# Recurrent scores with 64 stationary columns and a value half in groups of 512 columns: one kernel, two edits

## The chip, the cores and the metric

The kernel runs on one core of a Trainium2 chip. Its time is the device time of one execution in microseconds. The matrix engine (TensorE), the vector engine (VectorE), the scalar engine (ScalarE), GpSimd and the DMA queues run side by side and wait for each other through semaphores. In the rows below, PE is TensorE's matmul, PEld its loading of the stationary operand, DVE is VectorE, ACT ScalarE, POOL GpSimd, and SP the engine whose queue issues the loads.

## What is computed

One step of a two-layer decoder on 1024 prompt tokens and 64 sample tokens (8 sequences of 8), width 1024. Layer 0 has a convolution branch and a recurrent branch with 8 heads; layer 1 gates through a mixing of positions. Cut to the two places that the change touches:

```python
# layer 0, per head, chunks of 64 tokens: c = 64, n = 16
scores = jnp.einsum('bnthd,bnshd->bnhts', qf * jnp.exp(bcum - b_mid), k * jnp.exp(b_mid - bcum))
scores = jnp.where(causal, scores, 0.0)
o_intra = jnp.einsum('bnhts,bnshv->bnthv', scores, vf)

# layer 1: w_in is 1024 x 6144; columns 0..2047 are u, 2048..4095 are v, the rest the gate
z = _rmsnorm(x, g_norm) @ w_in
uv = jax.nn.gelu(z[..., :2 * D_C])
gate = z[..., 2 * D_C:]
u = uv[..., :D_C]
v = _layernorm(uv[..., D_C:], ln_g, ln_b)       # over the 2048 columns
mix = jnp.einsum('hts,bnshd->bnthd', ws, vp) + b_s
y = (u * mix * jax.nn.silu(gate)) @ w_out
```

## The kernel before

**Products.** Every large product is taken in float32r with both operands split into a high and a low part: three matmuls (high x high, high x low, low x high) for each of the 8 slices of the contraction. ScalarE makes the high part of a weight piece (`wh`), VectorE the low part (`wl`), from a raw piece of 512 KB that SP's queue loads. Two buffers hold raw pieces (pool `wrp`), three hold split pieces (pool `whp`), and `ft` is a pool of 31 large tiles for everything else. The list `wspecs` names the pieces in the order of use; `wget` takes the next ones and splits two (`AHEAD`) beyond them.

**Layer 0** is written in the order in which its instructions are to run. Weights are the stationary operand, and tokens stream in three pieces of 368, 352 and 368 columns. Between the pieces, generators add the small steps of the recurrent heads. `states(h, g)` does half `g` of head `h`: 512 tokens, four blocks of 128, each block two chunks of 64. For each block, one fp32 matmul makes the 128 x 128 scores of both chunks (line 729: 128 keys stationary, 128 queries moving) and a second one overwrites the corner in which the queries of the second chunk meet the keys of the first, with other scalings (line 730: 64 keys stationary, 64 queries moving). VectorE then copies the causal part into a tile that is zero elsewhere. `decode(h)` does the same for the sample tokens (line 790, 64 x 64), and for half 0 its scores stand right behind those of `states`.

**Layer 1's value half** begins once layer 0's output is summed. From here on a scheduler sets the order on all engines but SP, whose loads stay in the order of the text. Here the tokens are the stationary operand (128 of them) and the weights stream: `token_unit` (lines 503 to 505) takes a group of 256 weight columns as two pieces of 4 x 256 columns, and for each of 8 token blocks makes 24 matmuls with 256 columns into one PSUM tile. A ninth unit, the tail (lines 512 to 515), does the 64 sample tokens: a tile that holds their high and low parts side by side is stationary, and matmuls with 128 and with 64 stationary columns alternate. There are 8 groups. Each block is evacuated through a gelu on ScalarE and a statistics instruction on VectorE; four blocks make a tile that goes to DRAM (`va_d`, `vb_d`, and `vs_d` for the sample). After the first group a sum over columns is broadcast to all partitions (`rsqrt_bcast`, lines 1131 to 1133): three matmuls, three square roots on ScalarE, three reciprocals on VectorE. Later, `head_load(h)` loads the 256 columns of a head back, and the u and gate units of layer 1 run with weights stationary again.

**The end** (lines 1315 to 1317) is the one place that already takes weight pieces of 2 x 512 columns; those are kept in `ft` tiles (`fwh`, `fwl`).

Of the kernel before, what the change touches and what calls it, by code (L numbers as in the profile page):

```python
# [9 lines left out]
F32 = mybir.dt.float32  # L10
F32R = mybir.dt.float32r
I32 = mybir.dt.int32
AF = mybir.ActivationFunctionType
ALU = mybir.AluOpType

P = 128
# [4 lines left out]
NS = NSB * NSS  # L21
T = NPR + NS
KD = D // P
# [12 lines left out]
def kernel(  # L36
# [9 lines left out]
    cst = ctx.enter_context(tc.tile_pool(name="cst", bufs=1))  # L46
# [7 lines left out]
    def ft(name, dt=F32, shape=(P, T)):  # L54
        return ftp.tile(list(shape), dt, tag="ft", name=name)

    def ta(name, shape, dt=F32):
        return smp.tile(list(shape), dt, tag="a", bufs=5, name=name)
# [10 lines left out]
    def th(name, shape, dt=F32):  # L69
        return smp.tile(list(shape), dt, tag="h", bufs=6, name=name)  # L70

    def ps_mm(name):
        return mmp.tile([P, 512], F32, tag="mm", name=name)

    def ps_ax(name):
        return axp.tile([P, 512], F32, tag="ax", name=name)

    def dscr(name, n, w=T, p=P):
        return [tc.dram_tile([p, w], F32, name=f"{name}{i}") for i in range(n)]

    load = nc.sync.dma_start
    store = nc.scalar.dma_start
# [12 lines left out]
    tt_op = counted(nc.vector.tensor_tensor)  # L95
# [5 lines left out]
    act = nc.scalar.activation  # L101
    mm = nc.tensor.matmul
# [18 lines left out]
    w0, w1 = w_in_ab[0], w_in_c[0]  # L121
    wo0, wo1 = w_out_ab[0], w_out_c[0]
# [4 lines left out]

    def wload(spec):
        kind, w2d, rws, c0 = spec
        shape = {"u": [P, 8, P], "h": [P, 4, 256], "q": [P, 2, 512]}[kind]  # L130
        nk, nc_ = shape[1:]
        raw = wrp.tile(shape, F32, tag="wr", name="wr")
        load(out=raw, in_=w2d[rws * P:(rws + nk) * P, c0:c0 + nc_].rearrange("(k p) c -> p k c", p=P))
        return raw, shape

    def wsplit(rw, final=False):
        raw, shape = rw
        if not final:
            hi = whp.tile(shape, F32R, tag="wh", name="wh")
            lo = whp.tile(shape, F32R, tag="wl", name="wl")  # L140
        else:
            hi, lo = ft("fwh", F32R, shape), ft("fwl", F32R, shape)
        split(hi, lo, raw)
        return hi, lo

    VAL, GLU, AGT, QC, FC, IC, BGT = (1024 * i for i in range(7))
    wspecs = []
# [4 lines left out]
    def plan_h(w2d, c0, r0=0, n=2):  # L152
        for q in range(n):
            wspecs.append(("h", w2d, r0 + 4 * q, c0))
# [17 lines left out]
    for part in (2, 3, 0, 1):  # L172
        for mg in range(4):
            plan_h(wo0, mg * 256, 4 * part, 1)
    for g in range(8):
        plan_h(w1, 2048 + 256 * g)
    for h in range(8):
        for d in range(2):
            plan_u(w1, (2 * h + d) * P)
# [8 lines left out]
    wspecs = deque(wspecs)  # L188
# [11 lines left out]
    def wget(n=1, ahead=None):  # L200
        prefetch(n if here["manual"] else n + AHEAD)
        wuse[0] = n
        return [wready.popleft() for _ in range(n)]
# [183 lines left out]
    tail = ft("tail", F32R, (P, KD, P))  # L387
# [97 lines left out]
    def token_unit(ah, al, tail, evac):  # L485
# [43 lines left out]
        else:  # L529
            evac(8, NS, last())  # L530

    def act_evac(dst, func):
        return lambda a, n, ps: act(out=dst[:, a:a + n], in_=ps, func=func)

# [178 lines left out]
    def states(h, g):  # L713
        d = hd[h]
        k2, q2, sm, vr, o_t = d["k2"], d["q2"], d["sm"], vrows[h // 2], d["o"]
        hs = slice((h % 2) * P, (h % 2) * P + P)
        gs = slice(g * 512, (g + 1) * 512)
        for _ in range(g * LAG):
            yield
        q4, k3 = th("q4", [P, 8, 64]), th("k3", [P, 8, 64])  # L720
        for dst, src, r in ((k3, k2, 1), (q4, q2, 0)):
            tt_op(out=dst, in0=src[:, gs].rearrange("p (c s) -> p c s", s=64),
                  in1=sm[:, r, 8 * g:8 * g + 8, None].to_broadcast([P, 8, 64]), op=ALU.mult)
        for _ in range(LAG):
            yield
        sc = ps_ax("sc")
        for b in range(4):
            cs = slice((4 * g + b) * P, (4 * g + b + 1) * P)
            mm(sc[:, b * P:(b + 1) * P], k2[:, cs], q2[:, cs], start=True, stop=True)  # L729
            mm(sc[0:64, b * P + 64:(b + 1) * P], k3[:, 2 * b, :], q4[:, 2 * b + 1, :], start=True, stop=True)  # L730
        yield
        vpred(out=sct[g], mask=mcaus[:, None, :].to_broadcast([P, 4, P]),
              data=sc.rearrange("p (b t) -> p b t", b=4))
        for b in range(4):
            act(out=k3[:, 2 * b, :], in_=k3[:, 2 * b, :], func=AF.Copy, scale=sm[:, 2, 8 * g + 2 * b + 1:8 * g + 2 * b + 2])
        kp = ps_ax("kp")
        for b in range(4):
            nc.tensor.transpose(kp[:, b * P:(b + 1) * P],
                                k3[:, 2 * b:2 * b + 2, :].rearrange("p c s -> p (c s)"), ident)
        yield  # L740
        kt = th("kt", [P, 512])
        act(out=kt, in_=kp, func=AF.Copy)
        dp = ps_ax("dp")
        for b in range(4):
            mm(dp[:, b * P:(b + 1) * P], kt[:, b * P:(b + 1) * P], vr[4 * g + b][:, hs], start=True, stop=True)  # L745
        for b in range(4):
            act(out=q4[:, 2 * b + 1, :], in_=q4[:, 2 * b + 1, :], func=AF.Copy,
                scale=sm[:, 2, 8 * g + 2 * b:8 * g + 2 * b + 1])
        yield
        s_in = []  # L750
        for b in range(4):
            s_p = d.get("s")
            s_in.append(s_p)
            s_n = tb("Sn", [P, P])
            dpb = dp[:, b * P:(b + 1) * P]
            if s_p is None:
                vcopy(out=s_n, in_=dpb)
            else:
                stt(out=s_n, in0=s_p, scalar=sm[:, 3, 4 * g + b:4 * g + b + 1], in1=dpb,
                    op0=ALU.mult, op1=ALU.add)  # L760
            d["s"] = s_n
        op = ps_ax("op")
        for b in range(4):
            bs = slice(b * P, (b + 1) * P)
            mm(op[:, bs], vr[4 * g + b][:, hs], sct[g][:, b, :], start=True, stop=s_in[b] is None)  # L765
            if s_in[b] is not None:
                mm(op[:, bs], s_in[b], q4[:, 2 * b:2 * b + 2, :].rearrange("p c s -> p (c s)"),  # L767
                   start=False, stop=True)
        yield
        act(out=o_t[:, g * 512:(g + 1) * 512], in_=op, func=AF.Copy)  # L770
        if g == 1:
            store(out=hgrn_prompt[0, 0, h], in_=d["s"])
        d["done"] += 1
# [367 lines left out]
    rsqrt_cols(rc[0:NS, 8:9], mp[0:NS, 8:9], 1.0 / D)  # L1141
    rb = ft("rb")
    tail = tails(xh, xl)
    va_d = dscr("va_d", 8, 1024)
    vb_d = dscr("vb_d", 8, 1024)
    vs_d = dscr("vs_d", 8, 256, NS)
    bst = cst.tile([P, 9, 8, 6], F32, name="bst")
    for g in range(8):
        va = ft("va", F32, (P, 4, 256))
        vb = ft("vb", F32, (P, 4, 256))  # L1150
        vs = ta("vs", [NS, 256])

        def evac(t, n, ps):
            dst = vs if t == 8 else (va, vb)[t // 4][:, t % 4, :]
            act(out=dst, in_=ps, func=AF.Gelu_apprx_tanh, scale=rc[0:n, t:t + 1])
            nc.vector.bn_stats(out=bst[0:n, t, g, :], in_=dst)

        token_unit(xh, xl, tail, evac)
        store(out=va_d[g], in_=va.rearrange("p a b -> p (a b)"))
        store(out=vb_d[g], in_=vb.rearrange("p a b -> p (a b)"))  # L1160
        store(out=vs_d[g], in_=vs)
        if g == 0:
            rsqrt_bcast(rb, s2)
            s2 = None
# [15 lines left out]
    def head_load(h):  # L1180
        c0 = h * 256
        wst = smp.tile([P, P], F32, tag="st", bufs=4, name="wst")
        load(out=wst, in_=w_s[0, h])
        bsb = smp.tile([P, P], F32, tag="st", bufs=4, name="bsb")
        load(out=bsb, in_=b_s[0, h:h + 1, :].to_broadcast([P, P]))
        va = ft("va", F32, (P, 4, 256))
        vb = ft("vb", F32, (P, 4, 256))
        vs = tall("vs")
        load(out=va.rearrange("p a b -> p (a b)"), in_=va_d[h])
        load(out=vb.rearrange("p a b -> p (a b)"), in_=vb_d[h])  # L1190
        load(out=vs[0:NS, :], in_=vs_d[h])
        gb = [smp.tile([P, 256], F32, tag="gb", name="gb") for _ in range(2)]
        load(out=gb[0], in_=ln_c_g[0:1, c0:c0 + 256].to_broadcast([P, 256]))
        load(out=gb[1], in_=ln_c_b[0:1, c0:c0 + 256].to_broadcast([P, 256]))
        return wst, bsb, va, vb, vs, gb
# [99 lines left out]

    fg = ft("fg", F32, (P, D))
    load(out=fg, in_=final_norm[None, :].to_broadcast([P, D]))
    fw = [[wsplit(wload(("q", wo1, PARTS1[3][0] + 2 * q, 512 * c)), True) for q in range(2)] for c in range(2)]
    ss3 = cst.tile([P, 9, 3], F32, name="ss3")
    for t in range(9):  # L1300
        n = rows(t)
# [59 lines left out]
```

## Time and profile before

| | us |
|---|---|
| median of 3 runs | 1856.21 (1854.97 to 1856.58) |
| the profiled execution | 1856.37 |
| its span, first to last instruction | 1854.6 |
| TensorE busy | 1834.8 (99%) |
| VectorE busy | 1134.3 (61%) |
| ScalarE busy | 695.9 (38%) |
| mean granted clock of TensorE | 0.998 of full |

A busy sum counts a matmul from its start to its modelled end, and matmuls overlap: the next one starts before the one ahead has ended. So the share says that TensorE is never out of work, and not how fast it goes. How fast it goes stands in the starts: in a timeline, the distance from one start to the next is what a matmul costs the engine. In the timeline, records of one line that follow each other without a pause are drawn together (x2), and a narrow window separates them.

### The profile page before, as it was taken

What the parts mean: (1) busy time and instruction counts of PE and PEld (TensorE: products, weight loads), DVE (VectorE), ACT (ScalarE), POOL (GpSimd) and SP (SyncE); (2) the same over time, 40 slices, a digit from 0 to 9 for tenths busy, and PEclk for the clock granted to TensorE, in tenths of its full rate; (3) what the DMA queues carried; (4) which work ended last, traced back from release to release, by engine and by line L of the source; (5) the groups of instructions that cost most, each with busy time, mean ns of one, the idle gap of its engine ahead of it and who ended that gap; (6) DMA issues with size and microseconds to landing.
All of it is one profiled execution on the core that took longest, in us unless ns stands there. A gap on an engine that the chain in (4) does not pass through costs nothing.

```text
span 1854.6 us, 28644 instructions
## 1 busy us (share of the span) xinstructions
PE 1834.8 (99%) x12064; PEld 1802.3 (97%) x12064; DVE 1134.3 (61%) x1841; ACT 695.9 (38%) x1140; POOL 17.7 (1%) x50
## 2 busy tenths in 40 slices
PE   7999999999999999999999999999999999999998
PEld 6999999999999999999999999999999999999996
DVE  5468779878787868757786532245544545443435
ACT  5234442535254545545433422233232333320124
POOL 0000000000000000000000000000000000000000
PEclk9999999999999999999999999999999999999999
DMA  5112122213121313279333222244333321365402
GB/s 163 48 49 72 50 100 57 95 51 107 44 89 50 95 37 105 89 245 317 142 129 114 76 97 79 83 151 132 102 101 123 96 79 31 128 244 196 171 24 80
DMA packets 176673, 196.54 MB, mean 106 GB/s; under 512 B 7368, under 2 KB 151696, under 8 KB 176528
## 3 DMA queue, kind: packets, MB, share of 16 engines
q1 hardware_dynamic: 150952, 139.00, 23.8%
q10 hardware_dynamic: 25592, 55.71, 8.0%
q8 instruction: 95, 1.56, 0.4%
q14 instruction: 34, 0.28, 0.0%
HBM read 138.98 MB, written 56.42 MB: 105 GB/s over the span
## 4 chain that ended last, share of the span: by engine, by line
PE 98%; DVE 1%; ACT 0%; DMA 0%; issue 0%; SPq 0%; DVEq 0%; ACTq 0%
PE ps L465 23%; PE ps L467 22%; PE ps L466 22%; PE ps L504 5%; PE ps L503 5%; PE ps L505 5%; PE mp L1237 2%; PE sc L729 1%; PE sc L730 1%; PE ps L1317 1%; PE ps L1315 1%; PE ps L1316 1%; PE dp L745 1%; PE op L765 1%; PE op L825 1%; PE op L767 1%
## 5 line engine op out<-in xcount | busy, mean ns | idle before, releaser
L465 PE MATMUL ps<-xh,wh 128*128 128x368 f32 (+1 forms) x1080 | 356.7, 330 | 0.0
L467 PE MATMUL ps<-xh,wl 128*128 128x368 f32 (+1 forms) x1080 | 352.8, 327 | 0.0
L466 PE MATMUL ps<-xl,wh 128*128 128x368 f32 (+1 forms) x1080 | 352.7, 327 | 0.0
L92 DVE SCALAR_TENSOR_TENSOR y<-ab,cwt,y 128x1024 f32<-128x1024 f32 x240 | 307.4, 1281 | 0.2
L125 ACT ACTIVATE wh<-wr 128x1024 fp32r<-128x1024 f32 x132 | 139.0, 1053 | 348.4 <-PE ps L466 246.6
L92 DVE TENSOR_TENSOR wl<-wr,wh 128x1024 fp32r<-128x1024 f32 x132 | 161.2, 1221 | 152.4 <-ACT wh L125 152.2
L465 PE MATMUL ps<-gh,wh 128*128 128x368 f32 (+1 forms) x768 | 252.8, 329 | 0.0
L467 PE MATMUL ps<-gh,wl 128*128 128x368 f32 (+1 forms) x768 | 251.5, 327 | 0.0
L466 PE MATMUL ps<-gl,wh 128*128 128x368 f32 (+1 forms) x768 | 250.9, 327 | 0.0
L465 PEld LDWEIGHTS ps<-xh,wh 128*128 128x128 f32 x1080 | 202.7, 188 | 1.3
L466 PEld LDWEIGHTS ps<-xl,wh 128*128 128x128 f32 x1080 | 202.8, 188 | 0.3
L467 PEld LDWEIGHTS ps<-xh,wl 128*128 128x128 f32 x1080 | 202.8, 188 | 0.0
L92 DVE TENSOR_TENSOR x<-ps,x 128x368 f32<-128x368 f32 x168 | 88.6, 533 | 116.1 <-PE ps L467 113.4
L504 PE MATMUL ps<-wl,gh 128*128 128x256 f32 x512 | 145.4, 285 | 0.0
L505 PE MATMUL ps<-wh,gl 128*128 128x256 f32 x512 | 145.4, 285 | 0.0
L503 PE MATMUL ps<-wh,gh 128*128 128x256 f32 x512 | 144.8, 285 | 0.0
L465 PEld LDWEIGHTS ps<-gh,wh 128*128 128x128 f32 x768 | 144.2, 188 | 0.2
L466 PEld LDWEIGHTS ps<-gl,wh 128*128 128x128 f32 x768 | 144.2, 188 | 0.0
L467 PEld LDWEIGHTS ps<-gh,wl 128*128 128x128 f32 x768 | 144.2, 188 | 0.0
L465 PE MATMUL ps<-oh,wh 128*128 128x368 f32 (+1 forms) x384 | 127.6, 332 | 0.0
L467 PE MATMUL ps<-oh,wl 128*128 128x368 f32 (+1 forms) x384 | 125.5, 327 | 0.0
L466 PE MATMUL ps<-ol,wh 128*128 128x368 f32 (+1 forms) x384 | 125.4, 327 | 0.0
(311 smaller groups left out, 3383.2 us busy)
## 6 DMA issues: line engine op xcount, KB each, us to landing
wr<-in_w_in_ab_dram SPq DMA_DIRECT2D x56, 512.0 KB
wr<-in_w_in_c_dram SPq DMA_DIRECT2D x48, 512.0 KB
yr<-y_d SPq DMA_DIRECT2D x16, 544.0 KB
wr<-in_w_out_ab_dram SPq DMA_DIRECT2D x16, 512.0 KB
wr<-in_w_out_c_dram SPq DMA_DIRECT2D x16, 512.0 KB
yh_d<-yh ACTq DMA_DIRECT2D x12, 544.0 KB
yl_d<-yl ACTq DMA_DIRECT2D x12, 544.0 KB
oh<-yh_d SPq DMA_DIRECT2D x12, 544.0 KB
```

Source lines behind the costliest of these rows:

```text
L92: return f(**kw)
L125: act(out=hi, in_=src, func=AF.Copy)
L465: mm(ps[:, 0:cn], wh, ah[k][:, cs], start=(k == 0), stop=False)
L466: mm(ps[:, 0:cn], wh, al[k][:, cs], start=False, stop=False)
L467: mm(ps[:, 0:cn], wl, ah[k][:, cs], start=False, stop=(k == n_k - 1))
L503: mm(ps[:, 0:256], ah[k][:, ts], wh, start=(k == 0), stop=False)
L504: mm(ps[:, 0:256], ah[k][:, ts], wl, start=False, stop=False)
L505: mm(ps[:, 0:256], al[k][:, ts], wh, start=False, stop=(k == KD - 1))
L729: mm(sc[:, b * P:(b + 1) * P], k2[:, cs], q2[:, cs], start=True, stop=True)
L730: mm(sc[0:64, b * P + 64:(b + 1) * P], k3[:, 2 * b, :], q4[:, 2 * b + 1, :], start=True, stop=True)
L745: mm(dp[:, b * P:(b + 1) * P], kt[:, b * P:(b + 1) * P], vr[4 * g + b][:, hs], start=True, stop=True)
L1237: mm(mp[:, b * P:(b + 1) * P], vr[4 * g + b][:, ds_], wsT, start=True, stop=True)
```

## The change

**Scores.** For each block of 128 tokens, three matmuls with 64 stationary columns take the place of one with 128 and one with 64: the first chunk's keys with the first chunk's queries (64 x 64), the second chunk's keys with all 128 queries, written to PSUM partitions 64 to 127, and the same corner matmul as before.

**Value half.** Groups of 512 weight columns: 4 instead of 8. A group takes four pieces of 2 x 512 columns, every other one (`"qf"`) split into `ft` tiles instead of `whp` buffers. `token_wide` makes 24 matmuls with 512 columns for each token block. Two token blocks make a tile that is stored at once; `head_load` picks a head's 256 columns out of four such tiles.

```diff
-        shape = {"u": [P, 8, P], "h": [P, 4, 256], "q": [P, 2, 512]}[kind]
+        shape = {"u": [P, 8, P], "h": [P, 4, 256], "q": [P, 2, 512], "qf": [P, 2, 512]}[kind]
...
-    for g in range(8):
-        plan_h(w1, 2048 + 256 * g)
+    for g in range(4):
+        for q in range(4):
+            wspecs.append(("q" if q % 2 == 0 else "qf", w1, 2 * q, 2048 + 512 * g))
...
+    def token_wide(ah, al, tail, evac):
+        ws = wget(4)
+        def w(k):
+            return ws[k // 2][0][:, k % 2, :], ws[k // 2][1][:, k % 2, :]
+        for t in range(8):
+            ps = ps_mm("ps")
+            ts = slice(t * P, (t + 1) * P)
+            for k in range(KD):
+                wh, wl = w(k)
+                mm(ps, ah[k][:, ts], wh, start=(k == 0), stop=False)
+                mm(ps, ah[k][:, ts], wl, start=False, stop=False)
+                mm(ps, al[k][:, ts], wh, start=False, stop=(k == KD - 1))
+            evac(t, P, ps)
...
+        tl = th("tl", [NS, 512])
+        act(out=tl, in_=ps[NS:P, :], func=AF.Copy)
+        tt_op(out=tl, in0=ps[0:NS, :], in1=tl, op=ALU.add)
+        evac(8, NS, tl)
...
         for b in range(4):
-            cs = slice((4 * g + b) * P, (4 * g + b + 1) * P)
-            mm(sc[:, b * P:(b + 1) * P], k2[:, cs], q2[:, cs], start=True, stop=True)
+            c0 = (4 * g + b) * P
+            mm(sc[0:64, b * P:b * P + 64], k2[:, c0:c0 + 64], q2[:, c0:c0 + 64], start=True, stop=True)
+            mm(sc[64:P, b * P:(b + 1) * P], k2[:, c0 + 64:c0 + P], q2[:, c0:c0 + P], start=True, stop=True)
             mm(sc[0:64, b * P + 64:(b + 1) * P], k3[:, 2 * b, :], q4[:, 2 * b + 1, :], start=True, stop=True)
...
+                if t % 2 == 0:
+                    vq["w"] = ft("vq", F32, (P, 2, 512))
+                dst = vq["w"][:, t % 2, :]
...
+            elif t % 2 == 1:
+                store(out=v_d[g][t // 2], in_=vq["w"].rearrange("p a b -> p (a b)"))
...
-        load(out=va.rearrange("p a b -> p (a b)"), in_=va_d[h])
-        load(out=vb.rearrange("p a b -> p (a b)"), in_=vb_d[h])
-        load(out=vs[0:NS, :], in_=vs_d[h])
+        hs = slice((h % 2) * 256, (h % 2) * 256 + 256)
+        for q in range(4):
+            load(out=(va, vb)[q // 2][:, 2 * (q % 2):2 * (q % 2) + 2, :],
+                 in_=v_d[h // 2][q].rearrange("p (a b) -> p a b", a=2)[:, :, hs])
+        load(out=vs[0:NS, :], in_=vs_d[h // 2][:, hs])
```

On TensorE, the first two blocks of the first group of scores, between two projection pieces; in a row the moving operand stands ahead of the stationary one, `kk` holds the scaled keys and the last two numbers are stationary and moving columns. Before:

```order
L467 MATMUL ps<-xh_125,wl 128x352
L729 MATMUL sc<-q_1412,kk 128x128
L730 MATMUL sc<-q_1549,k_1550 64x64
L729 MATMUL sc<-q_1412,kk 128x128
L730 MATMUL sc<-q_1549,k_1550 64x64
```

```order
L468 MATMUL ps<-xh_125,wl 128x352
L760 MATMUL sc<-q_1412,kk 64x64
L761 MATMUL sc<-q_1412,kk 64x128
L762 MATMUL sc<-q_1549,k_1550 64x64
L760 MATMUL sc<-q_1412,kk 64x64
L761 MATMUL sc<-q_1412,kk 64x128
L762 MATMUL sc<-q_1549,k_1550 64x64
```

The second piece is the kernel after. Before, two matmuls a block alternate in width; now three stand there, all with 64 stationary columns, and the work ahead of and behind the group is the same.

On ScalarE, the end of the value half's first group: `wh` and `fwh` are splits of weight pieces, `tl` and `vs` the sample tail's evacuation, `rb` the broadcast norm. Before:

```order
L125 ACTIVATE wh_9851<-wr_9849 128x1024
L519 ACTIVATE tl_10088<-ps_10071 64x256
L1132 ACT_TABLE_LOAD
L1132 ACTIVATE rb_9797<-mp_10096,epsc_83 128x368
L1155 ACT_TABLE_LOAD
L1155 ACTIVATE vs_9842<-tl_10088,rc1_9790 64x256
L1132 ACT_TABLE_LOAD
L1132 ACTIVATE rb_9797<-mp_10100,epsc_83 128x352
L1161 DMA vs_d0_9831<-vs_9842 64x256
L1132 ACTIVATE rb_9797<-mp_10104,epsc_83 128x368
L125 ACTIVATE wh_10113<-wr_10111 128x1024
```

Here `wh_9851` is the second of group 1's two pieces, and `wh_10113` belongs to group 2. On the same engine and at the same place after the change:

```order
L125 ACTIVATE wh_10186<-wr_10184 128x1024
L558 ACTIVATE tl_10165<-ps_10148 64x512
L1164 ACT_TABLE_LOAD
L1164 ACTIVATE rb_9861<-mp_10172,epsc_83 128x368
L1189 ACT_TABLE_LOAD
L1189 ACTIVATE vs_10168<-tl_10165,rc1_9854 64x512
L1164 ACT_TABLE_LOAD
L1164 ACTIVATE rb_9861<-mp_10176,epsc_83 128x352
L1192 DMA vs_d0_9895<-vs_10168 64x512
L1164 ACTIVATE rb_9861<-mp_10180,epsc_83 128x368
L125 ACTIVATE fwh_10192<-wr_10190 128x1024
```

Now `wh_10186` is the third of group 1's four pieces and `fwh_10192` the fourth, so a piece of the very next group has moved behind the table loads and the square roots of the norm. On VectorE its low part stands behind the three reciprocals in the same way, after the change:

```order
L92 TENSOR_TENSOR wl_10187<-wr_10184,wh_10186 128x1024
L92 TENSOR_TENSOR tl_10165<-ps_10148,tl_10165 64x512
L1165 RECIPROCAL rb_9861<-rb_9861 128x368
L1190 BN_STATS bst_9899<-vs_10168 64x6
L1165 RECIPROCAL rb_9861<-rb_9861 128x352
L1165 RECIPROCAL rb_9861<-rb_9861 128x368
L92 TENSOR_TENSOR fwl_10193<-wr_10190,fwh_10192 128x1024
```

Before, the row in the last place was the low part of `wh_10113`, of group 2. On TensorE, the first token blocks of group 1 after the change (`ps_10208` is the first block's PSUM tile, `ps_10236` the second's, `ps_10264` the third's):

```order
L547 MATMUL ps_10236<-fwh_9920,gl3_9625 128x512
L545 MATMUL ps_10236<-wh_10186,gh4_9680 128x512
L545 MATMUL ps_10208<-fwh_10192,gh6_9786 128x512
L546 MATMUL ps_10236<-wl_10187,gh4_9680 128x512
L547 MATMUL ps_10236<-wh_10186,gl4_9681 128x512
L545 MATMUL ps_10236<-wh_10186,gh5_9730 128x512
L546 MATMUL ps_10236<-wl_10187,gh5_9730 128x512
L547 MATMUL ps_10236<-wh_10186,gl5_9731 128x512
L545 MATMUL ps_10236<-fwh_10192,gh6_9786 128x512
L545 MATMUL ps_10264<-wh_9914,gh0_9471 128x512
```

The scheduler has pulled the second block's matmuls, and then 9 of the third's, ahead of the rest of the first: 47 matmuls stand between the norm's last one and the first use of `fwl_10193`, where before each block of group 1 was finished before the next began.

## Rows read from the trace of the kernel before

**Rows 1.** The page: busy time of the engines, clock by slices, chain by engine.

```profile
PE 1834.8 (99%) x12064; PEld 1802.3 (97%) x12064; DVE 1134.3 (61%) x1841; ACT 695.9 (38%) x1140; POOL 17.7 (1%) x50
...
PEclk9999999999999999999999999999999999999999
...
PE 98%; DVE 1%; ACT 0%; DMA 0%; issue 0%; SPq 0%; DVEq 0%; ACTq 0%
```

**Rows 2.** Timeline of TensorE, first scores group: start us, us, engine, line, operation, tiles, stationary, moving.

```profile
159.19 0.38 PE L729 MATMUL sc<-q,kk 128*128 128x128 f32 x2
159.51 0.33 PE L730 MATMUL sc<-q,k 128*64 128x64 f32 x2
159.77 0.49 PE L729 MATMUL sc<-q,kk 128*128 128x128 f32 x2
...
160.44 0.49 PE L729 MATMUL sc<-q,kk 128*128 128x128 f32 x2
```

**Rows 3.** The same timeline in narrow windows, which show single records.

```profile
159.30 0.28 PE L729 MATMUL sc<-q,kk 128*128 128x128 f32 x1
...
161.64 0.22 PE L730 MATMUL sc<-q,k 128*64 128x64 f32 x1
161.70 0.28 PE L790 MATMUL sc<-q,kk 128*64 128x64 f32 x2
...
161.76 0.22 PE L790 MATMUL sc<-q,kk 128*64 128x64 f32 x1
161.91 0.44 PE L465 MATMUL ps<-xh,wh 128*128 128x368 f32 x1
```

**Rows 4.** Windows: stretch, length, busy us of each engine (records), clock, DMA share, GB/s.

```profile
1027.08:1231.70 204.62, 204.62 (x1689) 203.79 (x1688) 64.65 (x128) 63.87 (x107) 0.31 (x1) 0.99 0.27 91
1033.46:1035.40 1.94, 1.94 (x20) 1.93 (x18) 0.05 (x1) 0.00 (x0) 0.00 (x0) 1.00 0.00 0
1036.40:1039.80 3.40, 3.40 (x20) 3.40 (x19) 0.90 (x3) 2.48 (x4) 0.00 (x0) 0.54 0.02 5
```

**Rows 5.** Timeline of ScalarE, gelu evacuations of the value half's first group.

```profile
1048.27 0.47 ACT L1155 ACTIVATE vb<-ps,rc 128x256 f32<-128x256 f32 x1 [2.40 <-PE ps L505]
...
1054.03 0.48 ACT L1155 ACTIVATE vb<-ps,rc 128x256 f32<-128x256 f32 x1 [2.40 <-PE ps L505]
```

**Rows 6.** Timeline of TensorE, 512-column matmuls at the end of the kernel.

```profile
1791.92 0.39 PE L1317 MATMUL ps<-fwh,ol 128*128 128x512 f32 x1
...
1792.85 0.39 PE L1315 MATMUL ps<-fwh,oh 128*128 128x512 f32 x1
...
1838.13 0.39 PE L1316 MATMUL ps<-fwl,oh 128*128 128x512 f32 x1
...
1841.31 0.27 PE L1307 MATMUL pst<-ident,x 128*64 128x128 f32 x1
```

**Rows 7.** Timeline of TensorE, first and last matmul of a sample tail.

```profile
1130.34 0.28 PE L515 MATMUL ps<-wh,tail 128*128 128x256 f32 x1
...
1132.09 0.28 PE L515 MATMUL ps<-wh,tail 128*128 128x256 f32 x1
```

**Rows 8.** Timeline of TensorE, the norm's matmuls after the first group's tail.

```profile
1055.69 1.99 PE L1131 MATMUL mp<-sq,oner 128*128 128x368 f32 x6
1057.24 0.56 PE L503 MATMUL ps<-wh,gh 128*128 128x256 f32 x1
```

**Rows 9.** Timeline of ScalarE, the split behind the norm.

```profile
1062.35 1.06 ACT L125 ACTIVATE wh<-wr 128x1024 fp32r<-128x1024 f32 x1
```

**Rows 10.** Timeline of VectorE, reciprocals and the low part behind them.

```profile
1062.03 4.66 DVE L1133 RECIPROCAL rb<-rb 128x352 f32<-128x352 f32 x2 [0.96 <-ACT rb L1132]
1066.61 1.16 DVE L92 TENSOR_TENSOR wl<-wr,wh 128x1024 fp32r<-128x1024 f32 x1
```

**Rows 11.** Timeline of TensorE, steps in the stretch with the half clock.

```profile
1037.02 0.42 PE L503 MATMUL ps<-wh,gh 128*128 128x256 f32 x1
...
1039.80 0.41 PE L504 MATMUL ps<-wl,gh 128*128 128x256 f32 x1
```

More of the change, by code (lines that the diff above doesn't have):

```diff
@@ L133, in wload, with wsplit @@
         load(out=raw, in_=w2d[rws * P:(rws + nk) * P, c0:c0 + nc_].rearrange("(k p) c -> p k c", p=P))
[L134 to L138, printed above, removed]
+        return raw, shape, kind == "qf"
+    def wsplit(rw):
+        raw, shape, roomy = rw
+        if not roomy:
             hi = whp.tile(shape, F32R, tag="wh", name="wh")
@@ L530, in token_unit @@
             evac(8, NS, last())
+    def token_wide(ah, al, tail, evac):
[11 more added lines that the diff above has]
+            evac(t, P, ps)
+        ps = ps_mm("ps")
+        for k in range(KD):
+            wh, wl = w(k)
+            if k > 0:
+                mm(ps[0:NS, :], tail[:, k - 1, 0:NS], w(k - 1)[1], start=False, stop=False)
+            if k == KD - 1:
+                mm(ps[0:NS, :], tail[:, k, 0:NS], wl, start=False, stop=False)
+            mm(ps, tail[:, k, :], wh, start=(k == 0), stop=(k == KD - 1))
+        tl = th("tl", [NS, 512])
+        act(out=tl, in_=ps[NS:P, :], func=AF.Copy)
+        tt_op(out=tl, in0=ps[0:NS, :], in1=tl, op=ALU.add)
+        evac(8, NS, tl)
     def act_evac(dst, func):
@@ L1143 @@
     tail = tails(xh, xl)
[L1144 to L1151, printed above, removed]
-        def evac(t, n, ps):
-            dst = vs if t == 8 else (va, vb)[t // 4][:, t % 4, :]
+    v_d = [dscr(f"v{g}_d", 4, 1024) for g in range(4)]
+    vs_d = dscr("vs_d", 4, 512, NS)
+    bst = cst.tile([P, 9, 4, 6], F32, name="bst")
+    for g in range(4):
+        vq = {}
+        def evac(t, n, ps):
+            if t == 8:
+                dst = th("vs", [NS, 512])
+            else:
+                if t % 2 == 0:
+                    vq["w"] = ft("vq", F32, (P, 2, 512))
+                dst = vq["w"][:, t % 2, :]
             act(out=dst, in_=ps, func=AF.Gelu_apprx_tanh, scale=rc[0:n, t:t + 1])
             nc.vector.bn_stats(out=bst[0:n, t, g, :], in_=dst)
[L1158 to L1161, printed above, removed]
+            if t == 8:
+                store(out=vs_d[g], in_=dst)
+            elif t % 2 == 1:
+                store(out=v_d[g][t // 2], in_=vq["w"].rearrange("p a b -> p (a b)"))
+        token_wide(xh, xl, tail, evac)
         if g == 0:
@@ L1297 @@
     load(out=fg, in_=final_norm[None, :].to_broadcast([P, D]))
-    fw = [[wsplit(wload(("q", wo1, PARTS1[3][0] + 2 * q, 512 * c)), True) for q in range(2)] for c in range(2)]
+    fw = [[wsplit(wload(("qf", wo1, PARTS1[3][0] + 2 * q, 512 * c))) for q in range(2)] for c in range(2)]
     ss3 = cst.tile([P, 9, 3], F32, name="ss3")
```

## The prediction

> **What bounds the kernel now.** I read the page first, its busy line, its clock line and the chain that ended last [rows 1]: TensorE is busy 99% of the span and makes 98% of the chain, VectorE stands at 61% and ScalarE at 38%, and the granted clock reads 9, full, in every slice. Nearly every microsecond taken off TensorE therefore comes off the span, and every one added is paid, as long as the other engines still deliver in time. TensorE's instructions overlap (one takes 0.28 us and the next starts 0.12 us later), so a busy sum or a mean duration prices nothing here; the price of a matmul is the distance from its start to the next start. I read those distances from the timeline at the two places that the change touches, the scores and the value half, and then looked at what ScalarE and VectorE must deliver at a boundary of the value half.
>
> **Part one, the scores.** There are 8 heads x 2 halves = 16 groups of four blocks. Each fp32 matmul leaves two records. In a group of before [rows 2] a block, the 128-column matmul and then the 64-column one, starts at 159.77 and the next at 160.44: 0.67 us a block. Inside the block there is idle time that no other row has. From the second 128-column record of the first block at 159.30 to the first 64-column record at 159.51 [rows 2, 3] are 0.21 us, while the two 128-column records before stand 0.11 apart (159.19 and 159.30): 0.10 more. On the way out, the last 64-column record of the sample scores at 161.76 and the next projection matmul at 161.91 stand 0.15 apart, while 64-column records that follow each other (161.64, 161.70, 161.76) stand 0.06 apart: 0.09 more [rows 3]. So a change between 128 and 64 stationary columns in fp32 costs about 0.1 us each way, and before makes it eight times in a group. (The sample tail of the value half alternates the two widths in float32r without a pause, 0.117 a step [rows 7]; so it is not the width alone.)
>
> After the change all twelve matmuls of a group have 64 stationary columns. It enters the narrow form once and leaves it once (which before did too, at its last block). Block by block, two matmuls with 64 moving columns (A and C) have four records at 0.06 = 0.24 us, and the new one with 128 moving columns (B) two at 0.11 = 0.22, so 0.46 us. The entry costs the 0.10 above, and 0.05 for the first pair, whose first weight load nothing covers (in before, 159.51 to the next block's start at 159.77 is 0.26, the 0.15 of leaving and 0.11 instead of 0.06 for the pair). A group up to the sample scores is then 0.15 + 4 x 0.46 = 1.99 us, against 161.70 - 159.19 = 2.51 now [rows 2, 3]: 0.52 less, 8.3 us for 16 groups. The rows are rounded to 0.01; with the fast records at 0.057 instead of 0.06 it is 9.1. I take **8.8 us**. B writes to another half of the PSUM partitions than A and C, so its tile sits at another column position of the array; no row of before has that. Its cost is bounded on one side by the price of a change of width at each of its two ends (below, a loss) and on the other by running beside A and C (below, more gain). I take neither: nearest are the 64-column records at one position, which follow each other without a pause.
>
> That the PE order around the block is otherwise as before (the order rows of the first group show it) means nothing else of layer 0 moves. VectorE's mask copy reads the finished scores as it did, and VectorE and ScalarE have the slack of [rows 1].
>
> **Part two, the value half.** It runs from 1027.08 to 1231.70, with no idle time on TensorE and a clock of 0.99 [rows 4]. Two evacuations of one group, two tokens apart (1048.27 and 1054.03), stand 5.76 us apart for 48 matmuls with 256 columns: 0.120 us each [rows 5]. At the kernel's end the same kind of product already runs with 512 columns: from 1838.13 to 1841.31 are 14 steps, 0.227 us each [rows 6]. Two old ones take 0.240 and one new one 0.227, because of a fixed part of about 0.013 us a matmul. 1536 old matmuls become 768, so 768 x (0.240 - 0.227) = 9.9 us. The sample tail stays at 16 matmuls a group, in 4 groups instead of 8: 0.117 each now (1130.34 to 1132.09 are 15 steps, [rows 7]), 128 x 0.117 = 14.9 against 64 x 0.227 = 14.5, 0.4 us. Together **10.3 us**. The lower bound is the same line in its slow spell after the transposes, 1791.92 to 1792.85, 4 steps of 0.233 [rows 6]: 768 x 0.007 = 5.4 and nothing on the tail.
>
> Here a rule speaks against the change. The Trainium skill, TensorE: Matmul & The Clock Gate, section Back-to-back issue gap, gives the gap as N / 2.4 plus 2.5 ns, 262 cycles at 256 columns and 518 at 512; by it, as an estimate, halving the count saves only 768 x 2.5 ns = 2 us, where the rows give a fixed part of 13 ns.
>
> What must be in time: four weight pieces a group instead of two, the same bytes, the same number of splits. The tight place is the first boundary. In before the second piece of group 1 was split ahead of the table loads and reciprocals of the broadcast norm; now the fourth piece of group 1 (fwh_10192, fwl_10193 in the order rows) stands behind them on both engines. In the trace ScalarE reaches that place at 1062.35 and VectorE's last reciprocal ends at 1066.69, so a split there ends at 1067.77, 12.1 us after the tail's end at 1055.69 [rows 8 to 10]; the wider sample evacuations ahead add some 0.4 us. Against it stand the norm's matmuls, 1.55 us (1055.69 to 1057.24), and 47 matmuls of groups' first tokens that the order now puts ahead of the first use, 47 x 0.227 = 10.7: 12.3 us. That is a draw, a wait of 0 to 1 us; I take 0.2. Without the reordered tokens the first use would stand after 18 matmuls and TensorE would wait some 7 us. At the later boundaries three pieces are split long before, and the one that waits for a buffer has the rest of the tail and 12 matmuls as cover. The stores become 20 instead of 24 and off the path; the later loads of the heads go in four pieces with shorter runs on SP's queue, a whole head ahead of their use.
>
> **The sum.** 8.8 + 10.3 - 0.2 = 18.9 us. The profiled execution took 1856.4 (span 1854.6), the median of the three is 1856.2, so I put 1837.3 against the median, **1837**. The forecast's own range, from 5.4 to 10.3 on the value half and 8.3 to 9.1 on the scores, is 1836 to 1843.
>
> **Rivals.** *The tiles overlap.* If B runs beside A and C, a block falls below 0.46. If a weight load can only start once the matmul ahead of it has started, then only the second half of B is covered by the next load and record, 0.06 less a block; if nothing but the six records' pace of 0.057 bounds it, a block is 0.34. Times 64: 3.8 to 7.7 us more gain, **1829.6 to 1833.5**. For it: other positions of the array are free. Against it: no row shows two matmuls together. The Trainium skill, TensorE: Matmul & The Clock Gate, Part 3: Packing small matmuls, says that tiles at different positions run at the same time; no run here shows it yet.
>
> *A change of position drains like a change of width.* Then A to B and B to C cost 0.10 and 0.05 each, 0.30 a block, 19.2 us for 64: scores lose 10.4, the value half gives 10.1, **1856.5**, no change. The Trainium skill, TensorEngine Tiling (Array Packing), Key Properties, ties the drain to a change of mode and not of tile, which speaks against this one.
>
> *Weights late.* If every boundary waited 2 us and the stage's start too, 8 us go back: **1845**. The zero idle time and the scheduler's reordering speak against it, the draw above for it.
>
> *Time goes with the columns.* If a 512-column matmul took as long here as two of 256, 0.240, the value half would give nothing: 1856.2 - 8.8 = **1847.4**. Rows with 0.227 and 0.233 for the same kind of product speak against it [rows 6]. The gap of the Trainium skill quoted above comes near to this case and would end, as an estimate, 2 us below it.
>
> *The clock, the slower side.* At 1033.46 to 1035.40 TensorE did 1-column matmuls, and from 1036.40 to 1039.80 the granted clock was half (0.54 mean, 1.2 GHz), [rows 4]; the steps there were 13 in 2.78 us, 0.214 instead of 0.120 [rows 11], 1.5 us for 16 of them. If each new scores group, which leaves half of the columns empty, set off such a stretch, 16 x 1.5 = 24 us come back: **1861**. It decides from 13 of the 16 groups on. Against it: the old groups, with their pauses, kept the full clock.
>
> **How the numbers follow.** Forecast 0.45, overlap 0.36, late weights 0.06, draining positions 0.06, columns alone 0.03, clock 0.04. The range 1829 to 1843 takes in the forecast with its bounds and the overlap, 0.81. A measurement of this kernel can tell about 0.2%, 3.7 us: faster 0.90, same 0.06, slower 0.04.
>
> **What would show it.** In the profile after: one group of scores up to the sample scores in about 2.0 us (1.6 to 1.9 if tiles overlap, 3.2 if positions drain), the value half 10 us shorter with 0.227 us steps, PEclk full outside of the one stretch, no idle of TensorE on fwl. I am wrong if the group's length differs, or if TensorE idles at the boundary behind the reciprocals.

## The result and the profile after

| | before | after |
|---|---|---|
| median in the same comparison, us | 1855.59 (1854.84 to 1856.58, 4 runs) | 1823.92 (1821.65 to 1825.03, 4 runs) |
| profiled execution, us | 1856.4 | 1825.0 |
| its span, us | 1854.6 | 1823.2 |
| layer 0, first projection to the value half | 961.0 | 938.1 |
| value half | 204.8 | 194.5 |
| from there to the end | 622.8 | 623.2 |

The ratio is 0.9827, 95% interval 0.981 to 0.9844: 1.7% faster. Forecast was 1837, with a range of 1829 to 1843, so the time lies 5 us below the range. The value half gave 10.2 us, where the sum had 10.3; layer 0 gave 22.9 us where the sum had 8.8. These are 33.1, and the profiled executions differ by 31.4: 0.3 us went behind the value half, and 1.4 ahead of layer 0, where the first projection starts at 67.46 instead of 66.08. There after's granted clock was half (0.50, 1.2 GHz) for one stretch in which before's was full (1.00); matmuls with 416 columns started 0.35 us apart in it and 0.19 right behind it. No experiment below has this stretch, so it isn't counted to the change.

```profile
36.20:39.60 3.40, 3.40 (x11) 3.24 (x10) 0.69 (x2) 0.13 (x1) 0.00 (x0) 0.50 0.00 0
```

The page of after has the same bound as [rows 1]: TensorE 99% busy, the chain 98% TensorE.

```profile
PE 1803.2 (99%) x11360; PEld 1742.8 (96%) x11360; DVE 1126.8 (62%) x1801; ACT 682.8 (37%) x1100; POOL 18.0 (1%) x50
...
PE 98%; DVE 1%; ACT 1%; DMA 0%; issue 0%; ACTq 0%; SPq 0%; DVEq 0%
```

The first scores group, in narrow windows of TensorE's timeline (start us, us, engine, line, operation, tiles, stationary, moving); L760 is A (first chunk, 64 x 64), L761 is B (second chunk's keys, 128 queries, PSUM partitions 64 to 127), L762 is C (the corner), L822 the sample scores. It answers to [rows 2, 3].

```profile
160.66 0.27 PE L760 MATMUL sc<-q,kk 128*64 128x64 f32 x1
160.66 0.32 PE L761 MATMUL sc<-q,kk 128*64 128x128 f32 x1
160.76 0.22 PE L760 MATMUL sc<-q,kk 128*64 128x64 f32 x1
160.82 0.22 PE L762 MATMUL sc<-q,k 128*64 128x64 f32 x1
160.82 0.27 PE L761 MATMUL sc<-q,kk 128*64 128x128 f32 x1
160.88 0.22 PE L762 MATMUL sc<-q,k 128*64 128x64 f32 x1
160.93 0.27 PE L761 MATMUL sc<-q,kk 128*64 128x128 f32 x1
160.94 0.28 PE L760 MATMUL sc<-q,kk 128*64 128x64 f32 x2
...
161.52 0.28 PE L762 MATMUL sc<-q,k 128*64 128x64 f32 x2
161.64 0.28 PE L822 MATMUL sc<-q,kk 128*64 128x64 f32 x2
```

Read the lines L760 and L762 alone: 160.76, 160.82, 160.88, 160.94, a record every 0.058 us, as if L761 were not there. Read L761 alone: 160.66, then 160.82 and 160.93, from there on a record every 0.11. Two streams run at once. B's first record starts with A's first and 0.10 us ahead of A's second, although B stands behind A in the program. The group takes 161.64 - 160.66 = 0.98 us, where the forecast had 2.0 and the rival with overlap 1.6 to 1.9. (Their sums hold 0.10 us of way into the group, which lies ahead of its first record; like for like the measured group is 1.07.) TensorE's weight loads do the same; here B's first load starts 0.01 us behind A's:

```profile
160.65 0.13 PEld L760 LDWEIGHTS sc<-q,kk 128*64 128x64 f32 x1 [0.22 <-issue]
160.66 0.13 PEld L761 LDWEIGHTS sc<-q,kk 128*64 128x64 f32 x1
```

All 16 groups read alike: 0.981 us with the sample scores behind them and 1.075 without, where before took 2.507 and 2.606. That is 8 x 2.056 = 16.45 against 8 x 5.113 = 40.91, 24.5 less. The way into a group has become 0.09 us longer (0.254 and 0.203 from the last matmul ahead, instead of 0.162 and 0.109), 1.5 us for 16. The rest is 22.9, all that layer 0 lost.

The windows of after (stretch, length, busy us and records of PE, PEld, DVE, ACT, POOL, clock, DMA share, GB/s) answer to [rows 4]:

```profile
67.46:1005.54 938.08, 936.75 (x6395) 928.49 (x6394) 733.93 (x1118) 419.05 (x767) 3.17 (x14) 1.00 0.31 103
1005.54:1200.08 194.54, 194.54 (x857) 158.75 (x857) 57.97 (x88) 54.09 (x67) 0.00 (x0) 0.99 0.27 94
1015.80:1019.20 3.40, 3.40 (x9) 2.65 (x8) 0.36 (x3) 1.89 (x2) 0.00 (x0) 0.50 0.58 184
```

The value half has no idle time, and the one stretch with the half clock that before had too. ScalarE's evacuations in the value half now stand 5.44 us apart, one a token block (24 matmuls, 0.227 each), instead of two in 5.76 [rows 5]:

```profile
1025.83 0.69 ACT L1189 ACTIVATE vq<-ps,rc 128x512 f32<-128x512 f32 x1 [4.77 <-PE ps L547]
1031.27 0.69 ACT L1189 ACTIVATE vq<-ps,rc 128x512 f32<-128x512 f32 x1 [4.75 <-PE ps L547]
```

At the first boundary, after's tail ends where the norm's matmuls (L1163) begin, VectorE makes the low part of group 1's fourth piece (`fwl`) behind the last reciprocal, and TensorE comes to it after 47 matmuls. The rows answer to [rows 8, 10]:

```profile
1056.53 1.99 PE L1163 MATMUL mp<-sq,oner 128*128 128x368 f32 x6
```

```profile
1067.72 1.16 DVE L92 TENSOR_TENSOR fwl<-wr,fwh 128x1024 fp32r<-128x1024 f32 x1
```

```profile
1068.82 0.39 PE L547 MATMUL ps<-fwh,gl 128*128 128x512 f32 x1
1069.05 0.39 PE L546 MATMUL ps<-fwl,gh 128*128 128x512 f32 x1
```

The split ends at 1068.88, the first use starts at 1069.05, 0.23 behind the matmul ahead of it: 0.17 us to spare, and no wait.

### The profile page after: what moved, and what is told of

Read it like the earlier page. It is cut to its first block, busy times and chain, and to the rows that moved or that the text cites. A ratio compares the mean times of both kernels' runs of the same rounds, so it can differ in the third digit from the quotient of the medians.

```text
span 1823.2 us, 27162 instructions
## 1 busy us (share of the span) xinstructions
PE 1803.2 (99%) x11360; PEld 1742.8 (96%) x11360; DVE 1126.8 (62%) x1801; ACT 682.8 (37%) x1100; POOL 18.0 (1%) x50
## 4 chain that ended last, share of the span: by engine, by line
PE 98%; DVE 1%; ACT 1%; DMA 0%; issue 0%; ACTq 0%; SPq 0%; DVEq 0%
PE ps L466 23%; PE ps L468 23%; PE ps L467 23%; PE ps L547 3%; PE ps L545 3%; PE ps L546 3%; PE ps L504 2%; PE ps L505 2%; PE ps L506 2%; PE mp L1274 2%; PE ps L1354 1%; PE ps L1352 1%; PE ps L1353 1%; PE dp L777 1%; PE op L797 1%; PE op L857 1%
## 5 line engine op out<-in xcount | busy, mean ns | idle before, releaser
L125 ACT ACTIVATE wh<-wr 128x1024 fp32r<-128x1024 f32 x124 | 130.7, 1054 | 346.4 <-PE ps L467 248.1
L92 DVE TENSOR_TENSOR wl<-wr,wh 128x1024 fp32r<-128x1024 f32 x124 | 151.4, 1222 | 150.4 <-ACT wh L125 149.2
L92 DVE TENSOR_TENSOR g<-ps,rb 128x368 f32<-128x368 f32 (+1 forms) x48 | 25.7, 535 | 121.1 <-PE ps L468 121.1
L1190 DVE BATCH_NORM_STATS2 bst<-vq 128x6 f32<-128x512 f32 x32 | 22.0, 693 | 120.0 <-ACT vq L1189 120.0
L504 PE MATMUL ps<-wh,xh 128*128 128x256 f32 x256 | 72.9, 285 | 0.0
```

The lines of the kernel that those rows point to most:

```text
L92: return f(**kw)
L125: act(out=hi, in_=src, func=AF.Copy)
L504: mm(ps[:, 0:256], ah[k][:, ts], wh, start=(k == 0), stop=False)
```

## The experiments

Nine runs, each beside the kernel before on the same chip; they ran on three chips, on which the median of before was 1854.9 (s_only to s_width), 1855.0 (s_wide_a to s_runs, and merged) and 1856.2 (s_uncounted). "Group" is the first scores group up to the sample scores; "layer 0" as in the table above.

| run | median us | ratio to before (95%) | group | layer 0 | value half |
|---|---|---|---|---|---|
| s_only | 1832.17 | 0.9881 (0.9864 to 0.9897) | 0.982 | 938.2 | 203.3 |
| v_only | 1846.27 | 0.9951 (0.9936 to 0.9966) | 2.507 | 960.7 | 194.5 |
| s_pos0 | 1858.37 | 1.0016 (1.0006 to 1.0025) | 1.855 | 965.3 | 203.3 |
| s_width | 1839.02 | 0.9913 (0.9898 to 0.9928) | 1.498 | 944.8 | 203.3 |
| s_wide_a | 1839.73 | 0.9915 (0.9899 to 0.9932) | 1.388 | 944.7 | 203.3 |
| s_narrow_b | 1843.55 | 0.9936 (0.9921 to 0.9951) | 0.981 | 949.2 | 203.3 |
| s_runs | 1842.99 | 0.9932 (0.9917 to 0.9947) | (below) | 948.4 | 203.3 |
| s_uncounted | 1833.73 | 0.9879 (0.9863 to 0.9896) | 0.981 | 938.5 | 204.8 |
| merged | 1824.76 | 0.9835 (0.9821 to 0.985) | 1.915 for two | 940.0 | 194.6 |

### Each part alone

s_only is the kernel before with the scores' lines of the change and nothing else; v_only has all of the change but these lines.

> The scores edit alone, on the kernel before. Theory O (overlap: matmuls at two column positions run side by side, a block takes the longer of its two tiles): the scores groups as in the kernel after, 0.98 us up to the sample scores instead of 2.51, and 16 x (1.53 - 0.10 entry) = 22.9 us off layer 0: 1855.6 - 22.9 = 1832.7. Rival N (only the changes of width cost, position is of no account) expects the same here. If the two edits help or hinder each other, the time differs from 1832.7 by more than 3 us.

> The value half alone. By the stage lengths of the two traces (204.8 and 194.5 us) it takes 10.2 us off: 1845.4. The sum with the scores alone should be the whole gain of 31.7.

Measured: 1832.17 and 1846.27, against 1854.9 for before. 22.7 and 8.6 make 31.3, and the change as a whole 31.7: the parts add up. (Times of this kernel differ by 1.5 us from one execution to the next, last section, so 8.6 is not far from the 10.2 of the stage.) The scores alone overshot; the value half stands as forecast. The following runs take the scores apart; their edits are shown against s_only, that of s_width against the kernel before.

### B at the same column position

B goes to PSUM partitions 0 to 63 of a second tile, so all twelve matmuls have one position; VectorE copies the masked scores from two tiles, in two instructions.

```diff
+        sc2 = ps_ax("sc2")
...
-            mm(sc[64:P, b * P:(b + 1) * P], k2[:, c0 + 64:c0 + P], q2[:, c0:c0 + P], start=True, stop=True)
+            mm(sc2[0:64, b * P:(b + 1) * P], k2[:, c0 + 64:c0 + P], q2[:, c0:c0 + P], start=True, stop=True)
...
```

> Scores with 64 stationary columns as in the kernel after, but the 64 x 128 matmul also writes PSUM partitions 0 to 63 (of a second tile), so all three matmuls of a block sit at one column position; two mask copies instead of one. Value half as before. O: nothing overlaps, a block takes 0.46 us and a group up to the sample scores 1.9 to 2.0 us, gain 8 to 9 us: 1847, perhaps 1 or 2 us more if TensorE waits for the extra PSUM tile. N: a group takes 0.98 us as in the kernel after, 1833.

TensorE's timeline in s_pos0 (L730 is A, L731 B, L732 C):

```profile
159.29 0.33 PE L730 MATMUL sc<-q,kk 128*64 128x64 f32 x2
159.45 0.39 PE L731 MATMUL sc<-q,kk 128*64 128x128 f32 x2
159.68 0.28 PE L732 MATMUL sc<-q,k 128*64 128x64 f32 x2
159.79 0.28 PE L730 MATMUL sc<-q,kk 128*64 128x64 f32 x2
```

A stands in line behind C, and C behind B: from one A to the next 0.45 us where the two positions give 0.234. The same twelve matmuls cost 1.855 us a group at one position and 0.98 at two. The position is the cause of the overlap; it is worth 0.87 us a group, 14 us for 16. The total missed its expectation by far: layer 0 is 27 us longer than in s_only, 14 of them in the groups. The other 13 are not in the scores at all; two runs further on follow them.

### The pauses between widths

The old matmuls, in another order: in a group first the four with 128 stationary columns, then the four with 64.

```diff
         for b in range(4):
             cs = slice((4 * g + b) * P, (4 * g + b + 1) * P)
             mm(sc[:, b * P:(b + 1) * P], k2[:, cs], q2[:, cs], start=True, stop=True)
+        for b in range(4):
             mm(sc[0:64, b * P + 64:(b + 1) * P], k3[:, 2 * b, :], q4[:, 2 * b + 1, :], start=True, stop=True)
```

> The old matmuls (128 and 64 stationary columns), no new ones, but in each group the four wide ones first and then the four narrow ones: one change of width instead of seven inside the group. If a change of width costs what the rows of before gave (0.1 us each way and 0.05 to 0.1 for the pair behind it), a group up to the sample scores is 8 x 0.111 + 0.15 + 8 x 0.058 = 1.5 us, gain 16 us: 1839.6. If the pause belongs to something else (the corner that is written twice, say), it stays at 2.5 us: 1855.6.

```profile
159.26 1.05 PE L729 MATMUL sc<-q,kk 128*128 128x128 f32 x8
160.24 0.68 PE L731 MATMUL sc<-q,k 128*64 128x64 f32 x8
160.75 0.28 PE L791 MATMUL sc<-q,kk 128*64 128x64 f32 x2
```

160.75 - 159.26 = 1.49 us instead of 2.51. Six changes of width less are worth 1.0 us a group and 16 us of time, at no other cost. The prediction's price of a change (0.1 us on the way in, 0.1 on the way out, and a first pair with an uncovered load) is right. The run shows more: 16 of the 24.5 us that s_only took off the groups can be had by removing pauses alone, and with B at A's position the new matmuls (1.855) would be a worse answer to them than a new order of the old ones (1.498).

### What bounds a block: the longer position

A on all 128 queries: more columns, and position 0 has 2 x 0.11 + 2 x 0.058 = 0.334 us a block.

```diff
-            mm(sc[0:64, b * P:b * P + 64], k2[:, c0:c0 + 64], q2[:, c0:c0 + 64], start=True, stop=True)
+            mm(sc[0:64, b * P:(b + 1) * P], k2[:, c0:c0 + 64], q2[:, c0:c0 + P], start=True, stop=True)
```

> The scores edit alone, but the first matmul of a block takes 128 queries instead of 64 (the third overwrites its second half, as before). Theory O, that a block takes the longer of its two column positions: position 0 now has 2 x 0.109 + 2 x 0.058 = 0.334 us, position 64 still 0.218, so a block takes 0.334 and a group up to the sample scores 0.98 + 4 x 0.10 = 1.38 us; time 1832.2 + 16 x 0.40 = 1838.6. If the two shared one stream and a block cost a fixed share of their sum (0.45 to 0.56 us added up), the group would grow by the same fraction, to 1.21 us: 1836.

And B on its own 64 queries alone, which leaves position 64 half empty; its unwritten corner needs a mask copy in two instructions:

```diff
-            mm(sc[64:P, b * P:(b + 1) * P], k2[:, c0 + 64:c0 + P], q2[:, c0:c0 + P], start=True, stop=True)
+            mm(sc[64:P, b * P + 64:(b + 1) * P], k2[:, c0 + 64:c0 + P], q2[:, c0 + 64:c0 + P], start=True, stop=True)
...
+        vpred(out=sct[g][0:64], mask=mcaus[0:64, None, :].to_broadcast([64, 4, P]), data=scv[0:64])
+        vpred(out=sct[g][64:P, :, 64:P], mask=mcaus[64:P, None, 64:P].to_broadcast([64, 4, 64]),
+              data=scv[64:P, :, 64:P])
```

> The scores edit alone, with only 64 queries in the second matmul, and with the two mask copies (64 partitions x 512 and 64 partitions x 256) that the run with one position had, instead of one. O: position 0 is the longer one with 4 x 0.058 = 0.234 as it was, so a group stays at 0.98 us although a fifth of its columns is gone; a shared stream would make it shorter, about 0.75. The time tells the price of the second mask copy: 1832 if VectorE has room for it, about 1845 if it was the copies that cost the run with one position its 13 us.

From s_wide_a a whole block at position 0 (L730 is A, L732 C), then the first record of a group and the sample scores in s_narrow_b:

```profile
159.88 0.28 PE L730 MATMUL sc<-q,kk 128*64 128x128 f32 x1
...
159.99 0.27 PE L730 MATMUL sc<-q,kk 128*64 128x128 f32 x1
160.10 0.22 PE L732 MATMUL sc<-q,k 128*64 128x64 f32 x1
...
160.22 0.28 PE L730 MATMUL sc<-q,kk 128*64 128x128 f32 x1
```

```profile
159.42 0.27 PE L730 MATMUL sc<-q,kk 128*64 128x64 f32 x1
...
160.40 0.28 PE L794 MATMUL sc<-q,kk 128*64 128x64 f32 x2
```

In s_wide_a a group took 1.388 us, 0.334 for each of four blocks and 0.05 for the first load. Here C overwrites half of what A has just written, as the corner does in before, and there is no pause (two A records 0.11 apart, C 0.11 behind them): so before's pauses belong to the change of width and not to the corner that is written twice. In s_narrow_b the group stayed at 0.981: B's columns cost nothing. Both answers are those of two streams that don't slow each other, each with its own pace; the block ends with the longer one. But s_narrow_b's time is 11 us above s_only's.

### Where those 11 us went

TensorE's waits in s_narrow_b (engine, line, waited for, us in total, times, longest), those that s_only doesn't have:

```profile
PE ps L465 <- ACT ah L970: 1.7, 1, 1.7
PE mp L864 <- DVE sl L92: 1.3, 1, 1.3
PE ps L466 <- DVE al L92: 1.3, 2, 0.7
```

They stand at 800 to 950 us, where the convolution branch ends and layer 0 takes its norm. The last step of the convolution's sum on VectorE (`y<-y,y`; the times are of the first and the last of seven) comes at 810.2 instead of 786.0. First s_narrow_b, then s_only:

```profile
L92 DVE TENSOR_TENSOR y<-y,y x7: 1276/1284/1293, 249.4 to 810.2; 128x1088 f32<-128x1088 f32 x7
```

```profile
L92 DVE TENSOR_TENSOR y<-y,y x7: 1283/1291/1292, 248.6 to 786.0; 128x1088 f32<-128x1088 f32 x7
```

Two readings. Either VectorE's extra 16 copies of 0.45 us (7 us) push all behind them. Or the planner does: it counts each VectorE instruction's time (`clk["dve"]`) and lets the convolution go on only while that count lies behind TensorE's, so a copy that is counted holds the convolution back, whether or not VectorE is busy. In s_uncounted the second copy is issued without the count, and nothing else differs:

```diff
-        vpred(out=sct[g][64:P, :, 64:P], mask=mcaus[64:P, None, 64:P].to_broadcast([64, 4, 64]),
+        nc.vector.copy_predicated(out=sct[g][64:P, :, 64:P], mask=mcaus[64:P, None, 64:P].to_broadcast([64, 4, 64]),
```

> The kernel of s_narrow_b (the second mask copy for B's 64 queries), but this second copy is issued without being added to the planner's count of VectorE's time, so that the planner doesn't hold other VectorE work (the convolution taps) back for it. Theory 'the count': the 11 us that s_narrow_b lost against s_only come from the planner's count, which spread the taps over a longer time (last tap at 809.8 instead of 781.8 us); without it the last tap is back near 782 us and the time near s_only's, 1832 to 1834. Theory 'the engine': VectorE's real extra 7 us between 66 and 800 us push everything behind them; then the time stays at 1842 to 1845. Score groups 0.98 us in both.

Windows and the convolution's last step, first of s_narrow_b, then of s_uncounted:

```profile
66.00:800.00 734.00, 732.93 (x5142) 726.79 (x5142) 596.47 (x955) 333.27 (x669) 1.81 (x8) 1.00 0.25 79
800.00:950.00 150.00, 144.39 (x860) 140.34 (x859) 104.36 (x125) 64.18 (x77) 0.80 (x4) 0.97 0.60 209
```

```profile
66.00:800.00 734.00, 734.00 (x5151) 728.08 (x5150) 599.00 (x958) 333.68 (x670) 1.80 (x8) 1.00 0.26 81
800.00:950.00 150.00, 148.70 (x916) 146.34 (x916) 108.67 (x131) 65.06 (x79) 0.80 (x4) 1.00 0.58 202
```

```profile
L92 DVE TENSOR_TENSOR y<-y,y x7: 1284/1291/1293, 249.4 to 786.2; 128x1088 f32<-128x1088 f32 x7
```

With the same two copies, and VectorE a little busier ahead of 800 us (599.0), the last step is back at 786.2, TensorE's idle time between 800 and 950 falls from 5.6 to 1.3 us, the clock there is full again, and layer 0 takes 938.5. The planner's count was the cause, not the engine. What it cost in s_narrow_b is idle time for one half: 6.7 us from 66 to 950, where s_only has 1.2. The other half is the granted clock, which was half from 815.6 to 819.0 (0.50) and from 918.0 to 924.9 (0.51), in and behind these waits: TensorE was busy for 9.5 us of these stretches, so by estimate some 4.7 us were lost there. The 1.5 us by which s_uncounted's profile is longer than s_only's in the value half (204.8 and 203.3) come from the stretch of half clock that the last section shows. s_pos0 makes the same second copy and lost 13 us in the same place (its TensorE is busy for 142.71 of those 150 us at a clock of 0.95); that it is the count there too was not tried.

### How far B runs ahead

All A and C of a group first, then the four B:

```diff
-            mm(sc[64:P, b * P:(b + 1) * P], k2[:, c0 + 64:c0 + P], q2[:, c0:c0 + P], start=True, stop=True)
             mm(sc[0:64, b * P + 64:(b + 1) * P], k3[:, 2 * b, :], q4[:, 2 * b + 1, :], start=True, stop=True)
+        for b in range(4):
+            c0 = (4 * g + b) * P
+            mm(sc[64:P, b * P:(b + 1) * P], k2[:, c0 + 64:c0 + P], q2[:, c0:c0 + P], start=True, stop=True)
```

> The scores edit alone, with the eight matmuls at position 0 of all four blocks first and the four at position 64 behind them. If TensorE takes a ready matmul from far ahead in its queue, the group stays near 0.98 us. If it looks only a few instructions ahead (in the trace of the kernel after a matmul starts ahead of at most two or three that stand before it), the two runs add up: 0.05 + 16 x 0.058 + 8 x 0.109 = 1.85 us, as long as with one position, and the time is 1832.2 + 16 x 0.87 = 1846.

TensorE's timeline in s_runs (L730 is A, L731 C, L734 B); the first row is the 13th of 16 records of A and C:

```profile
160.12 0.22 PE L730 MATMUL sc<-q,kk 128*64 128x64 f32 x1
160.12 0.32 PE L734 MATMUL sc<-q,kk 128*64 128x128 f32 x1
160.18 0.22 PE L730 MATMUL sc<-q,kk 128*64 128x64 f32 x1
160.23 0.22 PE L731 MATMUL sc<-q,k 128*64 128x64 f32 x1
160.28 0.27 PE L734 MATMUL sc<-q,kk 128*64 128x128 f32 x1
160.29 0.22 PE L731 MATMUL sc<-q,k 128*64 128x64 f32 x1
```

B starts ahead of three records that stand before it, and no earlier; 12 of 16 ran alone. Layer 0 takes 10.2 us more than in s_only, 0.64 a group: less than the 0.87 expected, because these last records of A and C, and at the end the sample scores, still ran beside B. So matmuls of another position are taken ahead only over a short distance, three records here, and the order A, B, C inside a block is what keeps both streams fed.

### A step further

In the kernel after, both halves of a head take their scores in the same step, so that the narrow form is entered 8 times and not 16:

```diff
-        for _ in range(g * LAG):
-            yield
```

> The kernel after, with the two halves of a head in the same step, so that their score groups and the sample scores stand behind each other: one way into the narrow form and one out for each head instead of two. By the rows that is 0.15 and 0.20 us for 8 heads, 2.8 us: 1821 where the kernel after has 1823.9. If the two groups then wait for each other's PSUM tiles or for VectorE's copies, it is lost again: 1824 to 1830.

Measured 1824.76, no gain over after's 1823.92. The groups fell from 16.45 to 15.32 us in all, and eight ways into a group of 0.2 us are gone, but layer 0 is 940.0, 1.9 us longer: 4.6 us were lost again. TensorE now waits for the state that the second half takes from the first (L797), and once, later, for a tile `x`, which is 2.9 us of them; the rest is open:

```profile
PE op L797 <- DVE Sn L92: 1.9, 5, 0.6
...
PE ps L466 <- DVE x L92: 1.0, 1, 1.0
```

## Why the prediction was wrong

**The step that failed** is the choice for B: its cost "is bounded on one side by the price of a change of width ... and on the other by running beside A and C", and "I take neither: nearest are the 64-column records at one position". B was put in line, 0.46 us a block. s_pos0 shows that this price is right for one position (0.452). At another position B costs nothing: a block takes 0.234, and over 64 blocks that is the 14 us by which layer 0 gave more than forecast.

**The rival had the mechanism, but its floor was wrong too.** "The tiles overlap" stopped at 0.34 us a block because all six records were to share one pace of 0.057. Nothing is shared: A and C keep 0.058 and B 0.11 at the same time, weight loads included, and only the longer of the two counts (s_wide_a, s_narrow_b). From 0.34 to 0.234 are 6.8 us over 64 blocks, and with them the range would have reached down to 1823. (Two slips beside it: blocks of 0.34 to 0.40 make a group of 1.5 to 1.75 us by the prediction's own sum, not 1.6 to 1.9, and its bounds of 10.3 and 9.1 end at 1837, not 1836. Neither decides anything.) The argument against the rival, that no row showed two matmuls together, was no evidence: in before every matmul writes from PSUM partition 0 on, so nothing at a second position could have shown it. The Trainium skill, TensorEngine Tiling (Array Packing), Key Properties, states that different tiles can execute LdWeights and Matmul in parallel. The trace agrees: loads at 160.65 and 160.66, first records both at 160.66.

**Right, by their rows.** The price of a change of width: s_width measured 1.498 us a group. The value half: 768 steps of 0.227 for 1536 of 0.120; the block's distance gives 32 x (5.76 - 5.44) = 10.2, and the stage lost 10.2 in all. The rule that spoke for 2 us, the gap of the Trainium skill, TensorE: Matmul & The Clock Gate, Back-to-back issue gap, is given there for isolated matmuls and doesn't fit these rows; they decide. The tail's term was smaller: from 1052.83 to 1056.30 are 15 steps of 0.231, so 64 are 14.8 against the forecast's 14.9 for before, 0.1 us and not 0.4. The draw at the first boundary: the split ended 12.35 us after the tail and was used 12.52 after it (forecast 12.1 and 12.3).

**Rivals that fell.** Positions don't drain, the clock stayed full in layer 0 (1.00 over 938 us of after), the weights were in time, and 512 columns took less than two times 256.

**Right only just:** that VectorE has slack. It has, but s_narrow_b shows that the planner doesn't see it: 16 more counted copies cost 11 us there, a third of the change's gain.

## What to carry to other kernels

Small fp32 matmuls with 64 stationary columns whose outputs lie on different halves of the PSUM partitions run side by side when they alternate in program order; price a group by the longer of its two streams, and don't change between 64 and 128 stationary columns inside it. When no row of the profile can show a mechanism, its absence from the rows is no argument against it: let the range reach the bound where nothing is shared. And where a planner counts engine time, an instruction costs what the count makes of it, which can be more than the engine needs.

## What was not expected of the hardware

Matmuls at a second column position start ahead of up to three records that stand before them (s_runs), and their weight loads overlap.

The stretch with the half clock after the 18 one-column matmuls of the value half comes in some executions and not in others. In after they end at 1014.5, and the stretch stands at 1015.8 to 1019.2 (0.50). In the profile of s_only, where they end at 1012.5, the same stretch of time behind them has the full clock:

```profile
1013.50:1016.90 3.40, 3.40 (x31) 3.40 (x30) 1.16 (x3) 2.38 (x4) 0.00 (x0) 1.00 0.02 5
```

The value half takes 203.3 us without it and 204.8 with it, 1.5 us (s_only and s_uncounted, the same code there). The times of before lie in two heaps as far apart: in one comparison nine of 13 from 1854.7 to 1855.1, the other four from 1855.9 to 1856.5. That this stretch is what parts them is argued from its size, not shown for each run.
